# A depthwise convolution on VectorE: its two running sums get a PSUM bank each, and small operands move from SBUF to PSUM

## The chip, the cores and the metric

The kernel runs on one core of a Trainium2 chip. Its time is the device time of one execution in microseconds. TensorE, VectorE, ScalarE, GpSimd and SyncE each run their own instruction stream in order and meet through semaphores.

## What is computed

One inference step of a four-layer trunk, for a prompt of 512 tokens and for 8 samples of 4 tokens with shared weights, all in float32, D = 1024. Each layer is a mixer (pooling; Conformer convolution; chunked gating; short convolution) and a SwiGLU FFN of width 2816. The change is mostly in the second layer's mixer:

```python
def _rmsnorm(x, g):
    xf = x.astype(jnp.float32)
    y = xf * lax.rsqrt(jnp.mean(xf * xf, axis=-1, keepdims=True) + EPS)
    return (y * g.astype(jnp.float32)).astype(x.dtype)

def _conformer_conv(h, buf, w_in, b_in, dw, dw_b, ln_g, ln_b, w_out):
    z = jnp.einsum('bld,de->ble', h, w_in) + b_in
    a, gate = jnp.split(z, 2, axis=-1)
    g = a * jax.nn.sigmoid(gate)
    ext = jnp.concatenate([buf, g], axis=1)          # 30 earlier positions in front
    c = _depthwise_causal(ext, dw) + dw_b            # 31 taps per channel
    c = jax.nn.silu(_layernorm(c, ln_g, ln_b))
    return jnp.einsum('blc,cd->bld', c, w_out), ext[:, L:]

for i in range(DEPTH):
    h = _rmsnorm(x, norm_mix[i])
    x = x + mixer_i(h)
    x = x + _swiglu(_rmsnorm(x, norm_ffn[i]), ffn_w_in[i], ffn_w_out[i])
```

## The kernel before

Activations lie with channels on the 128 partitions and tokens along the free dimension: 8 chunks of 128 channels (`NC`), each with 544 token columns. The tokens are cut into half A (256 prompt tokens) and half B (256 prompt tokens and the 32 of the samples, 288 columns). Every float32 product is made of three matmuls from split operands: a rounded high part and the rest, `hi` and `lo`. Weights stream in through SyncE's queue (`raw`), ScalarE rounds them (`hi`, line 159), and VectorE or GpSimd subtracts (`lo`). Activations are split in the same way (`split`, `split_lo`: tiles `H_...`, `L_...`).

The order of each engine's instructions is that of the program text, which a planner writes: `Stream.run` walks over steps (a group of matmuls and its evacuation) and keeps a modelled clock per engine (`dve.t`, `pool.t`, `pe.t`; a VectorE instruction is taken to cost 0.07 us and 0.00104 us per element, `scalar_tensor_tensor` 0.065 more). Background jobs, the convolution's taps and norms among them, are generators that `background` advances after each step until `dve.t` reaches `pe.t` less a margin; a `yield None` waits for the next step. `settle` and `reached` hold a job back until the modelled clocks have passed. A step may also advance a job in its middle. `S.drain` issues what is left of the jobs.

The convolution of half A runs under the first layer's FFN of half B, and the convolution of half B under the second layer's FFN of half A. For each half:

- `conv_in` makes the gated inputs `ce` (tile `ext`) per chunk, 30 earlier columns in front; GpSimd clears or copies those columns. For half B `cs` holds the samples with their state.
- `conv_taps` adds 31 taps for the 256 prompt columns, in two running sums (even and odd taps) that lie in the two halves of one PSUM bank, `ct`. ScalarE writes the first tap of each; VectorE adds the other 29 with `scalar_tensor_tensor`, the last of the even ones into the SBUF tile `cc`, and then adds the odd sum to it. For the samples (half B), products with all 31 taps go into a bank `cw` and a `tensor_reduce` sums them; GpSimd adds the bias.
- GpSimd adds the finished `cc` of each chunk into `cm` (`accm`), for the mean over channels; the first chunk is copied there by ScalarE.
- `conv_norm` sums `cm` over partitions with a matmul (`cmean`), VectorE copies the mean to SBUF (`cmu`), subtracts it from each `cc`, ScalarE squares, GpSimd adds the squares (`cva`), and `token_rsqrt` makes the reciprocal root.

`token_rsqrt` sums over partitions into a bank `st_...`, so that tokens lie on partitions and a half has only two or three columns; `rsqrt_` then computes the root with shifts and Newton-like steps on VectorE in tiny SBUF tiles (`ms`, `ri`, `rt`); a matmul with the identity spreads the result over all partitions, into a bank `rp_...`. `scaled` has ScalarE copy that bank to SBUF (`r_...`, `cr`) with the constant factor `RSQ`. `Norm.prepare` then multiplies the eight chunks of x with the gain and `r` (`hn_...`), for the norms whose half is normalised before the matmuls (`pre`). The norms that take both halves at once use the same functions.

All PSUM tiles come from one pool of eight banks (`PS`, tag `ps`). A matmul group holds a bank from its first matmul to its evacuation.

In the profile, VectorE's and GpSimd's instructions carry line 102, that of the `Timed` helper, so they are told apart by tile.

Of the kernel before, what the change touches and what calls it, by code (L numbers as in the profile page):

```python
# [10 lines left out]
I32 = mybir.dt.int32  # L11
# [53 lines left out]
def trunk_kernel(  # L65
# [70 lines left out]
    def col(i):  # L136
        return colsT[:, i : i + 1]
# [200 lines left out]
            if gens:  # L338
                yield

    def rsqrt_(ms, shape_of, mk):

        wi, t = mk("ri"), mk("rt")
        wv, tv = shape_of(wi), shape_of(t)
        dve.tensor_scalar(wv.bitcast(I32), ms.bitcast(I32), 1, None, op0=ALU.logical_shift_right)
        dve.tensor_scalar(wv.bitcast(I32), wv.bitcast(I32), -1, 0x5F3759DF, op0=ALU.mult, op1=ALU.add)
        dve.tensor_mul(tv, wv, wv)
        dve.tensor_mul(tv, tv, ms)
        dve.scalar_tensor_tensor(wv, tv, -3.0, wv, op0=ALU.add, op1=ALU.mult)
        dve.scalar_tensor_tensor(tv, wv, 0.25, wv, op0=ALU.mult, op1=ALU.mult)  # L350
        dve.tensor_mul(tv, tv, ms)
        dve.scalar_tensor_tensor(tv, tv, -10.0 / 3, tv, op0=ALU.add, op1=ALU.mult)
        dve.scalar_tensor_tensor(wv, tv, 5.0, wv, op0=ALU.add, op1=ALU.mult)
        return wi

    def scaled(out, r):
        act.activation(out, r, AF.Copy, scale=RSQ)
# [1 line left out]
    def token_rsqrt(acc, halves, name, lag, mid=(None,)):  # L359

        bl = [b for b in range(5) if blocks[b][0] in halves]
        b0, b1 = bl[0], bl[-1] + 1
        ps = PS(f"st_{name}")
        ms = sp.tile([P, 5], F32, tag="nms", name=f"ms_{name}", bufs=2)
# [15 lines left out]
        rs = rsqrt_(  # L383
            ms[:, b0:b1], lambda t: t[:, b0:b1],
            lambda n: sp.tile([P, 5], F32, tag=f"n{n}", name=f"{n}_{name}", bufs=2),
        )
# [12 lines left out]

    class Norm:  # L400
# [277 lines left out]
    def pool_half(h):  # L678
# [15 lines left out]
        rs = rsqrt_(ms, lambda t: t, lambda n: sp.tile([P, nb], F32, tag=f"p{n}{h}", name=f"p{n}{h}"))  # L694
        if h == B:
            dve.tensor_scalar(rs, rs, RSQ, None, op0=ALU.mult)
        yield 2.5
# [148 lines left out]
    def conv_in(h, fill):  # L846
# [65 lines left out]
        for c in range(NC):  # L912
            la, lg = cols_of(w_cin[c], f"ci{c}_{h}", True)
            if c == 0:
# [5 lines left out]
            S.add([la], lambda wt, c=c: a_mm(wt, c), lambda ps, c=c: a_evac(ps, c),  # L920
                  fill=fill)

    def conv_taps(h, c, e, ev):
        w = HW[h]
        cc = cv[h][c] = T(f"cc_{h}_{c}")

        acc = PS(f"ct_{h}_{c}")
        outs = (acc[:, :HP], acc[:, HP : 2 * HP])
        for k in range(2):
            act.activation(  # L930
                outs[k], e[:, k : k + HP], AF.Identity, scale=col(C_DW + k * NC + c),
                bias=0.0 if k else col(C_DWB + c),
            )
        yield 0.0
        for k in range(2, CW):
            o = outs[k % 2]
            dve.scalar_tensor_tensor(
                cc[:, :HP] if k == CW - 1 else o, e[:, k : k + HP], col(C_DW + k * NC + c), o,
                op0=ALU.mult, op1=ALU.add,
            )  # L940
# [18 lines left out]
        if c == 0:  # L959
            accm[h] = T(f"cm_{h}")  # L960
            act.copy(accm[h][:, :w], cc[:, :w])
        else:
            pool.tensor_add(accm[h][:, :w], accm[h][:, :w], cc[:, :w])
        yield 0.7

    def conv_norm(h):
        w = HW[h]
        yield from settle()
        pm_ = PS(f"cmean_{h}")
        pe.matmul(pm_[:, :w], ones, accm[h][:, :w], start=True, stop=True)  # L970
        yield from reached()
        mu = T(f"cmu_{h}")
        dve.tensor_scalar(mu[:, :w], pm_[:, :w], 1.0 / D, None, op0=ALU.mult)
        av = T(f"cva_{h}")
# [12 lines left out]
        scaled(rs[:, :w], out[h][:, :w])
# [100 lines left out]
    def gm_norm():  # L1088
# [339 lines left out]
```

## Time and profile before

| | before |
|---|---|
| device time, median of 3 (lowest to highest) | 2260.37 us (2260.27 to 2268.2) |
| the profiled execution | 2267.77 us |
| its span, first to last instruction | 2266.1 us |
| mean granted TensorE clock in it | 0.982 |
| TensorE busy | 2185.4 us, 96% of the span |
| VectorE busy | 1361.7 us, 60% |
| ScalarE busy | 867.7 us, 38% |
| GpSimd busy | 541.0 us, 24% |

The profiled execution is one of the slower of those seen, 7.4 us over the median of the runs. The page gives shares and 40 slices of equal length; what follows also uses the busy time by stretch, the waits (who stood idle, until which instruction of which engine ended), the groups of like instructions and the timeline. An instruction's time in these views runs from its start to its end, and two on one engine can overlap a little.

### The profile page before, as it was taken

How to read it: one execution, taken by the hardware profiler on the slowest of the kernel's cores; microseconds unless marked ns; L12 is line 12 of the kernel's file. 1: busy time of each engine (PE TensorE's matmuls, PEld its weight loads, DVE VectorE, ACT ScalarE, POOL GpSimd, SP SyncE). 2: the span in 40 equal slices, each digit the busy share in tenths (PEclk: the TensorE clock that was granted, in tenths of full speed). 3: DMA queues.
4: the chain of work that ended last, by engine and by line, in shares of the span. 5: the costliest groups of instructions: out<-in, count | busy, mean ns of one | idle time of the engine just before them, and what ended most of it. 6: DMA issues, size and time to landing. Idle time of an engine off the chain costs nothing.

```text
span 2266.1 us, 41810 instructions
## 1 busy us (share of the span) xinstructions
PE 2185.4 (96%) x17110; PEld 2172.3 (96%) x17110; DVE 1361.7 (60%) x2569; ACT 867.7 (38%) x1407; POOL 541.0 (24%) x378
## 2 busy tenths in 40 slices
PE   9999988999788999999999999999999999999998
PEld 9999988999788899999999999999999999999998
DVE  6857789725999957566478543344465654433434
ACT  4445443454333465444434332232322233222322
POOL 3011666878667880000033000000000000000001
PEclk8999999999999999999999999999999999999999
DMA  6645543545654455555423322322344522232221
GB/s 228 219 146 165 170 140 113 176 151 170 144 151 140 167 168 171 152 190 149 141 79 126 106 83 70 110 92 68 93 89 95 94 84 94 67 97 98 88 71 60
DMA packets 112039, 284.07 MB, mean 125 GB/s; under 512 B 30540, under 2 KB 37800, under 8 KB 111584
## 3 DMA queue, kind: packets, MB, share of 16 engines
q1 hardware_dynamic: 110376, 279.47, 41.3%
q8 instruction: 134, 2.20, 0.4%
q10 hardware_dynamic: 1152, 1.32, 0.2%
q0 software_dynamic: 320, 0.62, 0.1%
q14 instruction: 57, 0.47, 0.1%
HBM read 277.11 MB, written 4.62 MB: 124 GB/s over the span
## 4 chain that ended last, share of the span: by engine, by line
PE 68%; DVE 10%; ACT 1%; issue 1%; DMA 1%; POOL 0%; DVEq 0%; POOLq 0%; ACTq 0%
PE ps_o L102 18%; PE ps_u L102 17%; PE ps_g L102 16%; DVE ct L102 3%; PE ps_gv L102 3%; PE ps_go L102 2%; PE ps_sc L102 2%; PE ps_sx L102 2%; PE ps_sbg L102 2%; PE ps_so L102 2%; PE ps_co L102 1%; DVE cw L102 1%; DVE cc L102 1%; DVE vT L102 1%; DMA raw_fi<-in_w_fin 0%
## 5 line engine op out<-in xcount | busy, mean ns | idle before, releaser
L102 DVE TENSOR_TENSOR lo_fi<-raw_fi,hi_fi 128x1024 fp32r<-128x1024 f32 (+1 forms) x180 | 222.1, 1236 | 333.2 <-issue 262.3
L159 ACT CAST hi_fi<-raw_fi 128x1024 fp32r<-128x1024 f32 x264 | 276.2, 1049 | 327.7 <-PE ps_g L102 108.3
L102 PE MATMUL ps_o<-H_p,lo_fo 128*128 128x288 f32 (+1 forms) x1408 | 354.8, 290 | 7.6 <-POOL lo_fo L102 7.6
L102 PE MATMUL ps_o<-H_p,hi_fo 128*128 128x288 f32 (+1 forms) x1408 | 355.7, 291 | 5.0 <-ACT H_p L507 5.0
L102 PE MATMUL ps_o<-L_p,hi_fo 128*128 128x288 f32 (+1 forms) x1408 | 355.5, 291 | 1.1 <-DVE L_p L102 1.0
L159 ACT CAST hi_fo<-raw_fo 128x768 fp32r<-128x768 f32 x192 | 150.0, 782 | 284.4 <-PE ps_o L102 150.1
L102 PEld LDWEIGHTS ps_o<-H_p,lo_fo 128*128 128x128 f32 x1408 | 249.7, 190 | 8.2 <-POOL lo_fo L102 8.2
L102 PEld LDWEIGHTS ps_o<-H_p,hi_fo 128*128 128x128 f32 x1408 | 250.0, 191 | 5.7 <-ACT H_p L507 5.7
L102 PEld LDWEIGHTS ps_o<-L_p,hi_fo 128*128 128x128 f32 x1408 | 250.0, 190 | 2.0 <-DVE L_p L102 2.0
L102 DVE TENSOR_TENSOR lo_fo<-raw_fo,hi_fo 128x768 fp32r<-128x768 f32 (+1 forms) x128 | 113.6, 890 | 226.3 <-issue 104.9
L102 PE MATMUL ps_u<-hH_f,hi_fi 128*128 128x256 f32 (+1 forms) x1040 | 242.4, 288 | 0.0
L102 PE MATMUL ps_g<-hH_f,hi_fi 128*128 128x256 f32 (+1 forms) x1040 | 242.4, 288 | 0.0
L102 PE MATMUL ps_g<-hL_f,hi_fi 128*128 128x256 f32 (+1 forms) x1040 | 242.4, 288 | 0.0
L102 PE MATMUL ps_u<-hL_f,hi_fi 128*128 128x256 f32 (+1 forms) x1040 | 242.3, 288 | 0.0
L102 PE MATMUL ps_g<-hH_f,lo_fi 128*128 128x256 f32 (+1 forms) x1040 | 241.7, 287 | 0.6 <-DVE lo_fi L102 0.6
L102 PE MATMUL ps_u<-hH_f,lo_fi 128*128 128x256 f32 (+1 forms) x1040 | 241.6, 287 | 0.0
L102 DVE SCALAR_TENSOR_TENSOR ct<-ce,colsT,ct 128x256 f32<-128x256 f32 x448 | 218.8, 488 | 24.3 <-ACT ct L930 11.2
L102 POOL TENSOR_TENSOR lo_fi<-raw_fi,hi_fi 128x1024 fp32r<-128x1024 f32 (+1 forms) x86 | 204.3, 2403 | 25.1 <-ACT hi_fi L159 21.5
L102 PEld LDWEIGHTS ps_g<-hH_f,lo_fi 128*128 128x128 f32 x1040 | 176.2, 188 | 0.8 <-DVE lo_fi L102 0.8
L102 PEld LDWEIGHTS ps_g<-hH_f,hi_fi 128*128 128x128 f32 x1040 | 176.2, 188 | 0.1
L102 PEld LDWEIGHTS ps_u<-hH_f,hi_fi 128*128 128x128 f32 x1040 | 176.2, 188 | 0.1
L102 PEld LDWEIGHTS ps_u<-hH_f,lo_fi 128*128 128x128 f32 x1040 | 176.2, 188 | 0.0
(346 smaller groups left out, 4922.6 us busy)
## 6 DMA issues: line engine op xcount, KB each, us to landing
raw_fi<-in_w_fin SPq DMA_DIRECT2D x264, 512.0 KB, 4.0
raw_fo<-in_w_fout SPq DMA_DIRECT2D x96, 384.0 KB, 3.2
raw_fo<-in_w_fout SPq DMA_DIRECT2D x96, 320.0 KB, 2.9
raw_ci<-in_w_cin SPq DMA_DIRECT2D x32, 512.0 KB, 4.0
raw_co<-in_w_cout SPq DMA_DIRECT2D x16, 512.0 KB, 4.8
raw_gi<-in_w_gin SPq DMA_DIRECT2D x16, 512.0 KB, 3.9
raw_go<-in_w_gout SPq DMA_DIRECT2D x16, 512.0 KB, 3.8
raw_si<-in_w_sin SPq DMA_DIRECT2D x16, 512.0 KB, 3.8
```

The costliest lines, as they stand in the source:

```text
L102: return fn(*a, **k)
L159: act.copy(self.hi, self.raw)
```

## The change

The convolution's two sums get a bank each, `ct0` and `ct1`. VectorE writes the first tap of each with `tensor_scalar`, with the bias in the first; ScalarE has no part in it any more. The two products for a pair of sample positions become one instruction of 2 × 8 × 31 elements, over a view with overlapping windows (`windows`). Adding a chunk to `cm` is put off (`late`) until the next chunk's twelfth tap has been issued; the last one is added at the start of `conv_norm`.

In `conv_norm` the mean is no longer copied: VectorE reads it from the bank `cmean` and scales and subtracts in one instruction. Each square is added one chunk later than before. In `conv_norm` and `Norm.prepare` the reciprocal root is read from its bank `rp_...` instead of an SBUF copy. The factor `RSQ` moves into that instruction or into a table of gains, which ScalarE scales once at the start (`gains`, 72 columns).

`rsqrt_` takes, for the norms of one half, two more column ranges in the bank `st_...` (`twin`). The two integer shifts stay in SBUF; of each later instruction at most one tensor operand is in SBUF, and three small copies keep both places filled. The norms of both halves and those of the first and third layers' mixers compute as before, except that the first shift writes the other of the two tiles.

```diff
-    def rsqrt_(ms, shape_of, mk):
-        wi, t = mk("ri"), mk("rt")
-        wv, tv = shape_of(wi), shape_of(t)
-        dve.tensor_scalar(wv.bitcast(I32), ms.bitcast(I32), 1, None, op0=ALU.logical_shift_right)
-        dve.tensor_scalar(wv.bitcast(I32), wv.bitcast(I32), -1, 0x5F3759DF, op0=ALU.mult, op1=ALU.add)
-        dve.tensor_mul(tv, wv, wv)
-        dve.tensor_mul(tv, tv, ms)
...
+    def rsqrt_(ms, wv, tv, twin=None):
+        wp, tp = twin or (wv, tv)
+        def copied(dst, src):
+            if twin:
+                dve.tensor_copy(dst, src)
+        dve.tensor_scalar(tv.bitcast(I32), ms.bitcast(I32), 1, None, op0=ALU.logical_shift_right)
+        dve.tensor_scalar(wv.bitcast(I32), tv.bitcast(I32), -1, 0x5F3759DF, op0=ALU.mult, op1=ALU.add)
+        copied(wp, wv)
+        dve.tensor_mul(tp, wv, wp)
+        dve.tensor_mul(tp, tp, ms)
+        dve.scalar_tensor_tensor(wp, tp, -3.0, wv, op0=ALU.add, op1=ALU.mult)
+        copied(wv, wp)
+        dve.scalar_tensor_tensor(tp, wp, 0.25, wv, op0=ALU.mult, op1=ALU.mult)
+        dve.tensor_mul(tp, tp, ms)
+        copied(tv, tp)
+        dve.scalar_tensor_tensor(tp, tp, -10.0 / 3, tv, op0=ALU.add, op1=ALU.mult)
+        dve.scalar_tensor_tensor(wv, tp, 5.0, wv, op0=ALU.add, op1=ALU.mult)
...
+        twin = (ps[:, 8 + b0 : 8 + b1], ps[:, 16 + b0 : 16 + b1]) if len(halves) == 1 else None
...
-            r = T(f"r_{nm}")
-            scaled(r[:, :w], out[h][:, :w])
+            r = out[h]
...
-                        v, x[h][:, i, :], col(self.g + i), r[:, :w], op0=ALU.mult, op1=ALU.mult
+                        v, x[h][:, i, :], gains[:, self.g + i : self.g + i + 1], r[:, :w],
+                        op0=ALU.mult, op1=ALU.mult,
...
+    act.activation(gains, colsT[:, :C_FIN], AF.Copy, scale=RSQ)
...
     def conv_taps(h, c, e, ev):
-        acc = PS(f"ct_{h}_{c}")
-        outs = (acc[:, :HP], acc[:, HP : 2 * HP])
-        for k in range(2):
-            act.activation(outs[k], e[:, k : k + HP], AF.Identity, scale=col(C_DW + k * NC + c), bias=...)
-        yield 0.0
-        for k in range(2, CW):
-            o = outs[k % 2]
-            dve.scalar_tensor_tensor(cc[:, :HP] if k == CW - 1 else o, e[:, k : k + HP], col(...), o, ...)
+        outs = [PS(f"ct{i}_{h}_{c}")[:, :HP] for i in range(2)]
+        for k in range(CW):
+            o = outs[k % 2]
+            wk = col(C_DW + k * NC + c)
+            src = e[:, k : k + HP]
+            if k == 0:
+                dve.tensor_scalar(o, src, wk, col(C_DWB + c), op0=ALU.mult, op1=ALU.add)
+            elif k == 1:
+                dve.tensor_scalar(o, src, wk, None, op0=ALU.mult)
+            else:
+                dve.scalar_tensor_tensor(cc[:, :HP] if k == CW - 1 else o, src, wk, o, op0=ALU.mult, op1=ALU.add)
+            if k == 11 and late:
+                late.pop()()
             if k % 2:
                 yield 0.8
...
-                for i in range(2):
-                    pv = b3(pr[:, i * DB * CW : (i + 1) * DB * CW])
-                    dve.tensor_mul(pv, ev[:, :, t + i : t + i + CW], taps)
+                pv = pr[:, : 2 * DB * CW].rearrange("p (i b k) -> p i b k", i=2, b=DB)
+                dve.tensor_mul(pv, windows(ev, t), taps)
...
-            pool.tensor_add(accm[h][:, :w], accm[h][:, :w], cc[:, :w])
+        late.append(gather)                  # gather() holds the copy or add into accm
...
     def conv_norm(h):
+        late.pop()()
...
-            dve.tensor_sub(cc, cc, mu[:, :w])
+            dve.scalar_tensor_tensor(cc, pm_[:, :w], -1.0 / D, cc, op0=ALU.mult, op1=ALU.add)
...
-            dve.tensor_mul(cc, cc, rs[:, :w])
+            dve.scalar_tensor_tensor(cc, cc, RSQ, out[h][:, :w], op0=ALU.mult, op1=ALU.mult)
```

More of the change, by code (lines that the diff above doesn't have):

```diff
@@ L366, in token_rsqrt @@
         ps = PS(f"st_{name}")
-        ms = sp.tile([P, 5], F32, tag="nms", name=f"ms_{name}", bufs=2)
+        ms, rs, tv = (sp.tile([P, 5], F32, tag=f"n{n}", name=f"{n}_{name}", bufs=2) for n in ("ms", "ri", "rt"))
+        twin = (ps[:, 8 + b0 : 8 + b1], ps[:, 16 + b0 : 16 + b1]) if len(halves) == 1 else None
         if B in halves:
@@ L382, in token_rsqrt @@
                 )
[L383 to L386, printed above, removed]
+        rsqrt_(*(t[:, b0:b1] for t in (ms, rs, tv)), twin)
         yield from lag
@@ L664, in trunk_kernel @@
     act.dma_start(colsT, par)
+    gains = cp.tile([P, C_FIN], F32, tag="gains", name="gains")
     wpool = [Load(w_pool[:, i], 1024, f"pool{i}") for i in range(2)]
@@ L693, in pool_half @@
         dve.scalar_tensor_tensor(ms, ms, EPS, mv[:, :, 1], op0=ALU.add, op1=ALU.add)
-        rs = rsqrt_(ms, lambda t: t, lambda n: sp.tile([P, nb], F32, tag=f"p{n}{h}", name=f"p{n}{h}"))
+        wv, tv = (sp.tile([P, nb], F32, tag=f"p{n}{h}", name=f"p{n}{h}") for n in ("ri", "rt"))
+        rs = wv
+        rsqrt_(ms, wv, tv)
         if h == B:
@@ L921, in conv_in, with windows @@
                   fill=fill)
+    late = []
+    def windows(ev, t):
+        v = ev[:, :, t : t + CW]
+        p, b, k = v.ap
+        return bass.AP(tensor=v.tensor, offset=v.offset, ap=[p, [1, 2], b, k])
     def conv_taps(h, c, e, ev):
@@ L925, in conv_taps @@
         cc = cv[h][c] = T(f"cc_{h}_{c}")
-        acc = PS(f"ct_{h}_{c}")
-        outs = (acc[:, :HP], acc[:, HP : 2 * HP])
-        for k in range(2):
[L930 to L933, printed above, removed]
-        yield 0.0
-        for k in range(2, CW):
-            o = outs[k % 2]
[L937 to L940, printed above, removed]
+        outs = [PS(f"ct{i}_{h}_{c}")[:, :HP] for i in range(2)]
+        for k in range(CW):
+            o = outs[k % 2]
+            wk = col(C_DW + k * NC + c)
[5 more added lines that the diff above has]
+            else:
+                dve.scalar_tensor_tensor(
+                    cc[:, :HP] if k == CW - 1 else o, src, wk, o, op0=ALU.mult, op1=ALU.add
+                )
+            if k == 11 and late:
+                late.pop()()
             if k % 2:
@@ L943, in conv_taps @@
         if ev is not None:
-            taps = colsT[:, C_DW + c : C_DW + CW * NC : NC].unsqueeze(1).to_broadcast([P, DB, CW])
+            taps = colsT[:, C_DW + c : C_DW + CW * NC : NC].unsqueeze(1).unsqueeze(1).to_broadcast([P, 2, DB, CW])
             for t in range(0, DS, 2):
                 pr = PS(f"cw_{c}_{t}")
-                for i in range(2):
-                    pv = b3(pr[:, i * DB * CW : (i + 1) * DB * CW])
-                    dve.tensor_mul(pv, ev[:, :, t + i : t + i + CW], taps)
+                pv = pr[:, : 2 * DB * CW].rearrange("p (i b k) -> p i b k", i=2, b=DB)
+                dve.tensor_mul(pv, windows(ev, t), taps)
                 dve.tensor_reduce(
                     b3(cc[:, HP:w]).rearrange("p b t -> p t b")[:, t : t + 2, :],
-                    pr[:, : 2 * DB * CW].rearrange("p (i b k) -> p i b k", i=2, b=DB),
+                    pv,
                     axis=mybir.AxisListType.X, op=ALU.add,
@@ L958, in conv_taps, with gather @@
         dve.tensor_add(cc[:, :HP], cc[:, :HP], outs[1])
[L959 to L962, printed above, removed]
-            pool.tensor_add(accm[h][:, :w], accm[h][:, :w], cc[:, :w])
+        def gather():
+            if c == 0:
+                accm[h] = T(f"cm_{h}")
+                act.copy(accm[h][:, :w], cc[:, :w])
+            else:
+                pool.tensor_add(accm[h][:, :w], accm[h][:, :w], cc[:, :w])
+        late.append(gather)
         yield 0.7
@@ L971, in conv_norm @@
         yield from reached()
-        mu = T(f"cmu_{h}")
-        dve.tensor_scalar(mu[:, :w], pm_[:, :w], 1.0 / D, None, op0=ALU.mult)
         av = T(f"cva_{h}")
-        sq = []
+        last = None
         for c in range(NC):
             cc = cv[h][c][:, :w]
-            dve.tensor_sub(cc, cc, mu[:, :w])
+            dve.scalar_tensor_tensor(cc, pm_[:, :w], -1.0 / D, cc, op0=ALU.mult, op1=ALU.add)
             s = av if c == 0 else T(f"csq_{h}_{c}")
             act.activation(s[:, :w], cc, AF.Square)
-            if c:
-                pool.tensor_add(av[:, :w], av[:, :w], s[:, :w])
+            if last is not None:
+                pool.tensor_add(av[:, :w], av[:, :w], last[:, :w])
+            last = s if c else None
             yield 0.4
+        pool.tensor_add(av[:, :w], av[:, :w], last[:, :w])
         yield from settle()
         out = yield from token_rsqrt({h: av}, (h,), f"cln_{h}", settle(), reached())
-        rs = T(f"cr_{h}")
-        scaled(rs[:, :w], out[h][:, :w])
         yield from reached()
@@ L1094, in gm_norm @@
         dve.tensor_scalar(ms, mv[:, :, 1], EPS, None, op0=ALU.add)
-        rs = rsqrt_(ms, lambda t: t, lambda n: sp.tile([P, 5], F32, tag=f"g{n}", name=f"g{n}"))
+        wv, tv = (sp.tile([P, 5], F32, tag=f"g{n}", name=f"g{n}") for n in ("ri", "rt"))
+        rs = wv
+        rsqrt_(ms, wv, tv)
         dve.tensor_scalar(rs, rs, RSQ, None, op0=ALU.mult)
```

6 lines of the change are left out of this document (removed).

## The prediction

> **What bounds the kernel now.** I read the page's shares and its 40 slices first.
>
> ```profile
> PE 2185.4 (96%) x17110; PEld 2172.3 (96%) x17110; DVE 1361.7 (60%) x2569; ACT 867.7 (38%) x1407; POOL 541.0 (24%) x378
> PE   9999988999788999999999999999999999999998
> DVE  6857789725999957566478543344465654433434
> POOL 3011666878667880000033000000000000000001
> PEclk8999999999999999999999999999999999999999
> ```
>
> TensorE is the bound over the whole, and no part of the change takes a convolution matmul away. What can be won are the slices where PE falls to 7 or 8. Most lie at slices 4 to 14, where VectorE shows 9 and GpSimd 6 to 8: the two convolutions under the FFN halves. Next, the busy time by stretch; each pair is busy us (instructions), then the granted clock:
>
> ```profile
> core 0: us, PE busy (x) PEld busy (x) DVE busy (x) ACT busy (x) POOL busy (x), PEclk, DMA share, GB/s
> 265.00:400.00 135.00, 119.39 (x866) 117.05 (x865) 121.67 (x267) 54.01 (x84) 89.97 (x57) 0.95 0.41 131
> 400.00:480.00 80.00, 76.76 (x567) 76.24 (x566) 51.17 (x74) 41.70 (x69) 63.57 (x33) 0.98 0.52 171
> 480.00:520.00 40.00, 40.00 (x304) 40.00 (x303) 5.51 (x12) 16.54 (x27) 31.08 (x20) 1.00 0.52 152
> 560.00:765.00 205.00, 172.86 (x1315) 170.43 (x1313) 190.31 (x365) 81.73 (x124) 139.31 (x87) 0.93 0.56 150
> 765.00:840.00 75.00, 71.29 (x566) 70.38 (x567) 51.16 (x66) 44.09 (x81) 64.86 (x37) 0.95 0.50 152
> 840.00:1160.00 320.00, 320.00 (x2467) 319.52 (x2466) 189.16 (x331) 145.64 (x227) 11.49 (x15) 1.00 0.50 156
> ```
>
> Where no convolution runs (840 to 1160) PE is full at clock 1.00. In W1, the taps of half A (265 to 400), it idles 135 − 119.4 = 15.6 us and loses 5% of 119.4 = 6.0 to the lower clock; it needs 113.4. In W2, the taps of half B (560 to 765), it idles 32.1 and loses 7% of 172.9 = 12.1; it needs 160.8. Together 65.8 us are lost, and VectorE is busy 90 and 93% there. The tails (400 to 480, 765 to 840) lose 3.2 + 1.5 and 3.7 + 3.6. That total, 78 us, is the ceiling.
>
> Then what PE waited for in W2 and, last three rows, around W1 (265 to 420): total, times, longest.
>
> ```profile
> PE ps_u L102 <- DVE cc L102: 9.1, 3, 4.5
> PE ps_gu L102 <- DVE ce L102: 8.3, 1, 8.3
> PE ps_o L102 <- POOL lo_fo L102: 4.3, 1, 4.3
> PE rp_f L102 <- DVE ri_f L102: 4.0, 1, 4.0
> ...
> PE ps_u L102 <- POOL lo_fi L102: 2.8, 1, 2.8
> PE ps_gu L102 <- POOL ce L102: 2.5, 1, 2.5
> PE ps_ca L102 <- POOL lo_ci L102: 1.1, 1, 1.1
> ```
>
> Half of W2 is VectorE late; in W1 it is GpSimd. But GpSimd is itself held, in order, by the channel sum `cm`, and each channel's taps begin with a wait for ScalarE (around W1, then in W2):
>
> ```profile
> POOL cm L102 <- DVE cc L102: 27.6, 6, 6.9
> POOL cm L102 <- PE ps_g L102: 6.4, 1, 6.4
> DVE ct L102 <- ACT ct L930: 7.2, 4, 2.5
> DVE ct L102 <- ACT ct L930: 4.0, 3, 1.6
> ```
>
> **The taps, each sum in its own bank.** VectorE's timeline and the groups by shape (busy us, mean ns, idle before):
>
> ```profile
> 339.66 4.17 DVE L102 SCALAR_TENSOR_TENSOR ct<-ce,colsT,ct 128x256 f32<-128x256 f32 x8 [1.52 <-ACT ct L930]
> 343.73 0.45 DVE L102 TENSOR_TENSOR L_p<-ps_u,H_p 128x288 fp32r<-128x288 f32 x1
> 344.10 3.10 DVE L102 SCALAR_TENSOR_TENSOR ct<-ce,colsT,ct 128x256 f32<-128x256 f32 x6
> ...
> L102 DVE SCALAR_TENSOR_TENSOR ct<-ce,colsT,ct 128x256 f32<-128x256 f32 x448 | 218.8, 488 | 24.3 <-ACT ct L930 11.2
> L102 DVE TENSOR_SCALAR sy<-se,colsT 128x256 f32<-128x256 f32 x16 | 5.6, 347 | 0.0
> ```
>
> Eight taps of 490 ns end after 4.17 us, so they start 525 ns apart: each begins 35 ns after the one before has ended. The unrelated `L_p` starts 4.07 us after the first tap, 4.07 − 7 × 0.525 = 0.395 after the last one, which is still running. So VectorE starts an instruction that needs nothing from its predecessor 0.13 us earlier. The sums alternate: tap k needs the result of k−2, and the only thing it shares with k−1 is the bank. With two banks, k−2 is 0.79 us back and has ended. How many pairs? The idle of the `ct` row without ScalarE's part is 24.3 − 11.2 = 13.1 us; at 35 ns that is 374 gaps, 187 per half. Each gives 0.127 us: 23.8 us per half.
>
> VectorE also takes on the first two taps, 16 × 2 instructions from SBUF into PSUM. No row has that form. The nearest, `sy`, is 0.35; with the overlap seen above it could be 0.26, and a full tap costs 0.40. I take 0.36: 5.8 us per half, bounds 4.2 and 6.4. By the Trainium skill, "VectorE: DVE Perf Modes", section "Why PSUM operands drop a tier", fp32 with PSUM runs one element per cycle; an estimate from its 0.96 GHz, 256 cycles, is 4.3 us per half before any fixed part. In return the waits for ScalarE go, 7.2 and 4.0. Late next is then whatever ScalarE waited for: the rows `ce` (VectorE's own, in order) and GpSimd's copy of the carried columns, priced below.
>
> **Sample products, norms, means.** These have in common that operands leave SBUF.
>
> ```profile
> L102 DVE TENSOR_TENSOR cw<-cs,colsT 128x248 f32<-128x248 f32 x32 | 28.9, 903 | 0.5
> L102 DVE TENSOR_TENSOR cw<-cs,colsT x32: 608/648/2658, 594.6 to 761.9; 128x248 f32<-128x248 f32 x32
> L102 DVE TENSOR_TENSOR cc<-cc,cmu 128x288 f32<-128x288 f32 x8 | 11.1, 1449 | 0.0
> L102 DVE TENSOR_TENSOR cc<-cc,cr 128x288 f32<-128x288 f32 x8 | 9.6, 1204 | 0.8 <-ACT cr L357 0.8
> L102 DVE SCALAR_TENSOR_TENSOR y<-xg,rp_nl 128x288 f32<-128x288 f32 x8 | 3.0, 446 | 1.9 <-PE rp_nl L102 1.9
> L102 DVE SCALAR_TENSOR_TENSOR hn_f<-x,colsT,r_f 128x256 f32<-128x256 f32 x8 | 5.7, 748 | 0.0
> 572.48 2.30 DVE L102 TENSOR_SCALAR ri_f<-ri_f 128x2 int32<-128x2 int32 x1
> 574.82 0.16 DVE L102 TENSOR_TENSOR rt_f<-ri_f 128x2 f32<-128x2 f32 x1
> 575.80 2.24 DVE L102 SCALAR_TENSOR_TENSOR rt_f<-rt_f 128x2 f32<-128x2 f32 x1
> ```
>
> Two columns take 0.16 us or 2.3, and `cc` 1.2 to 1.4 us where the same 288 columns with one PSUM operand (`y`) take 0.45. The long ones lie where GpSimd is busy; I read them as instructions held while GpSimd works on SBUF.
> - `cw`: two products become one of 496 columns. The pair costs 2 × 0.903 = 1.81. The new one lies between 0.9 (the time per column of the plain rows, plus one hold of 0.26) and 1.6 (2 × 0.648 plus that hold); I take 1.37, since 608 ns as the shortest of 248 columns says that it is slow by itself. 16 × 0.44 = 7 us in W2, bounds 3 and 14.
> - `hn_f` from PSUM: 748 to the taps' 488, eight times: 2.1 us in W2.
> - The norm at 572: the two shifts stay in SBUF, so the 2.30 stays; the 2.24 falls to 0.16; three copies of 0.2 are added: 1.5 us. Other one-half norms gain a hold or two, or lose 0.6 where GpSimd is idle; at the very start and end that may show, so −1 for all.
> - The means: `mu`'s instruction goes, and the 16 `cc` of a half fall to 0.45: 8 × (1.00 + 0.76) = 14 us of VectorE in B's tail, and as much in A's. PE loses only 12 us in both tails, so most of this is worth nothing; with two norms of `n1` nearby I take 5 us.
> - ScalarE loses 32 taps and a scale per norm; at 38% busy that shows nowhere but in the waits already counted. `gains` runs in a ScalarE that is idle until the first split: nothing, unless the parameter load lands late (0.5 us).
> - The banks of the norm are held for its eight products instead of one copy, and a channel holds two of eight banks instead of one; TensorE groups queue for the rest. In the sum nothing; a rival below.
>
> **GpSimd's sums later.** `cm` is issued after tap 11 of the next channel, some 5 us after what it reads is done. So the 27.6 + 6.4 us in which GpSimd stood before its `lo` splits go, and with them W1's waits for `lo_fi` and `lo_fo`. B's `cc` bias still follows the sample reduction at once, so there the queue stays held whenever VectorE is late. GpSimd's lateness at W1's start (`ce` 2.5, `lo_ci` 1.1) has no such cause and stays: with its share of the clock loss (6.0 on 15.6) 5 us.
>
> **The sum.** W1: VectorE is freed of 23.8 + 7.2 − 5.8 = 25.2 us and needs 110 where PE needs 113.4. PE leads again: its 21.6 lost us come back but for the 5, that is 16 us. W2: 23.8 + 4.0 + 7.0 + 2.1 + 1.5 − 5.8 = 32.6, VectorE still needs 172 against PE's 160.8 and sets the pace: 33 us. Tails and norms 5, copies −1: 53 us in all. The profiled execution took 2267.8 (span 2266.1); less 53 that is 2215. The median of the runs, 2260.4, is 7.4 lower, so I say 2207. With the bounds (taps −1 to +3, `cw` −4 to +7, tails 0 to 10) this case runs from 2190 to 2225.
>
> **Rivals.**
> 1. The 525 ns do not come from the bank: they are what dependent-looking instructions cost. The Trainium skill ("VectorE: DVE Perf Modes", "The DRAIN you can't avoid") says the next operation "does not start until the 8-stage pipe empties", semaphore or not. By that rule the 47.6 us of both halves stay. The `L_p` row, 0.395 us behind a tap of 490, speaks against it. Then W1 gains 7.2 − 5.8 = 1 us, W2 9, GpSimd's freed queue some 5, tails 4: 19 us, 2241.
> 2. Banks: `ps_u <- DVE cc` (9.1 us in 3) looks like TensorE waiting for a bank that the sums held. With one bank fewer it meets this more often, though VectorE, now on time, releases sooner. Eight more such waits of 3 us with the clock loss give back 30: 2237.
> 3. Slower: the same mechanism at every channel. A wait at 9.1 / 3 = 3.0 us plus 1.2 of lost clock, at both banks of 16 channels, is over 130 us; at one bank of each, 67: 2260 − 53 + 67 = 2274. It decides from 3.3 us per channel (53 / 16) on. Against it: before, PE shows three such waits in W2 and none around W1.
> 4. Better: VectorE's relief in W2 passes on whole and the clock stays up; nearly the ceiling of 78: 2182.
>
> **Chances.** Forecast 0.58; rival 1, 0.1; rival 2, 0.13; rival 3, 0.05; rival 4, 0.14. The range takes rivals 2 and 4 in: 2180 to 2240. 0.5%, or 11 us, is about what can be told from no change here; faster has rivals 1, 2, 4 and the forecast but for a rest near zero: 0.9, same 0.05, slower 0.05.
>
> **What would show it.** Taps start about 0.40 us apart and none waits for ScalarE; the two starting taps are near 0.36. In W1 and W2 PE at 95% or more and clock near 1.00, VectorE at 80 to 95%. No `cm` wait on VectorE; the `cc` bias wait remains, shorter. `cc` near 0.45, the norm's ten middle steps all at 0.16 with two shifts still long. Wrong if taps stay at 525 ns, if PE waits for `cc` grow, or if GpSimd's `lo` become what PE waits for in W2.

## The result and the profile after

| | before | after |
|---|---|---|
| median (lowest to highest) | 2262.51 us (2260.27 to 2268.2), 4 runs | 2192.11 us (2191.2 to 2195.81), 4 runs |
| ratio, 95% interval | | 0.9688 [0.9665, 0.9711] |
| profiled execution, its span | 2267.77, 2266.1 us | 2191.2, 2189.3 us |

The change takes 70 us off. The profile's page after the change, in the rows that the prediction showed of before:

```profile
PE 2156.0 (98%) x17110; PEld 2147.0 (98%) x17110; DVE 1298.7 (59%) x2613; ACT 851.4 (39%) x1372; POOL 542.7 (25%) x378
PE   9999999999999999999989999999999999999997
DVE  7867798517999566565587443344555554434444
POOL 3011787888788910000050000000000000000001
PEclk9999999999999999999999999999999999999998
```

TensorE's holes in slices 4 to 14 (the first slice is 0) are gone. The 9s of VectorE in slices 10 to 12 are the convolution of half B, where it is still the slower engine.

**By stretch.** The convolution is best cut at TensorE's own marks, since the stretches of fixed length shift. A runs from the first `ps_cga` matmul of half A to its first `ps_co` matmul, B from there to the first `ps_co` matmul of half B. Busy time by stretch, before and then after; the columns are the prediction's, and the first row of each pair is A:

```profile
238.98:527.82 288.84, 267.93 (x1988) 264.47 (x1987) 195.83 (x376) 128.94 (x201) 210.88 (x126) 0.97 0.47 150
527.82:848.55 320.73, 283.45 (x2197) 278.93 (x2196) 273.19 (x470) 145.09 (x236) 238.37 (x144) 0.95 0.55 154
```

```profile
232.33:491.83 259.50, 257.48 (x1989) 257.03 (x1987) 169.66 (x397) 122.07 (x184) 211.77 (x126) 1.00 0.53 167
491.83:773.28 281.45, 270.91 (x2197) 267.61 (x2195) 233.11 (x477) 135.47 (x216) 239.66 (x144) 0.99 0.62 175
773.28:2189.30 1416.02, 1399.07 (x11044) 1395.34 (x11042) 721.10 (x1396) 475.38 (x778) 51.61 (x65) 0.99 0.35 103
```

A gives 29.3 us, B 39.3, and what follows B 1.5 (1417.55 before): together 70. The two profiles differ by 6.7 us more, because the first convolution matmul came at 238.98 us before and at 232.33 after. Over all profiles of this study, whose code ahead of that point is nearly the same, it came between 231.4 and 239.0, so this is not counted as the change's. The late start would also account for the profiled execution of before lying 5.3 us above its median; the other executions left no profile. The 1.5 us behind B are within what the profiles of the experiments differ by there (1415.8 to 1419.6 us), so they cannot be called the change's either.

**By the prediction's stretches**, at the places to which they have moved and a little wider in matmuls: W1, A's tail, W2, B's tail, with what TensorE waited for longest in W2:

```profile
258.00:375.00 117.00, 117.00 (x908) 117.00 (x907) 112.60 (x287) 50.11 (x71) 97.13 (x60) 1.00 0.53 165
375.00:470.00 95.00, 95.00 (x722) 94.94 (x721) 39.61 (x77) 48.21 (x81) 74.43 (x39) 1.00 0.53 165
518.00:700.00 182.00, 172.57 (x1384) 170.73 (x1383) 176.29 (x372) 76.19 (x110) 148.56 (x88) 0.99 0.65 175
700.00:780.00 80.00, 78.88 (x648) 77.63 (x648) 44.60 (x79) 50.28 (x90) 68.13 (x43) 1.00 0.59 181
```

```profile
PE ps_gu L102 <- DVE ce L102: 2.8, 1, 2.8
PE ps_ca L102 <- DVE cc L102: 1.6, 1, 1.6
PE ps_g L102 <- DVE cc L102: 1.5, 1, 1.5
PE ps_g L102 <- POOL lo_fi L102: 1.4, 1, 1.4
```

W1 and A's tail lose nothing any more: TensorE is busy for 117.00 of 117 and 95.00 of 95 us at clock 1.00. W2 still loses 9.4 us of idle time and 1% of 172.6 to the clock, 11 in all, against 44 before; there VectorE is busy for 176 of 182 us. B's tail loses 1. So of the 78 us that the prediction called the ceiling, 66 came back; the other 3 of A's and B's gain lie ahead of W1 and W2.

**On VectorE.** Its timeline in half B's taps, and its groups by shape:

```profile
561.44 0.93 DVE L102 TENSOR_SCALAR ct<-ce,colsT 128x256 f32<-128x256 f32 x2
562.29 4.00 DVE L102 SCALAR_TENSOR_TENSOR ct<-ce,colsT,ct 128x256 f32<-128x256 f32 x10
566.20 0.23 DVE L102 SCALAR_TENSOR_TENSOR cs<-ps_ca,colsT,ct 128x32 f32<-128x32 f32 x1
...
L102 DVE SCALAR_TENSOR_TENSOR ct<-ce,colsT,ct 128x256 f32<-128x256 f32 x448 | 182.1, 480 | 0.0
L102 DVE TENSOR_TENSOR cw<-cs,colsT 128x496 f32<-128x496 f32 x16 | 28.6, 1790 | 0.0
L102 DVE TENSOR_SCALAR ct<-ce,colsT 128x256 f32<-128x256 f32 x32 | 14.9, 510 | 0.1
L102 DVE TENSOR_TENSOR L_cn<-cc,H_cn 128x256 fp32r<-128x256 f32 x8 | 11.5, 1450 | 2.7 <-ACT H_cn L512 2.7
L102 DVE SCALAR_TENSOR_TENSOR cc<-cc,rp_cln 128x288 f32<-128x288 f32 x8 | 3.4, 441 | 0.0
```

Ten taps fill 566.20 − 562.29 = 3.91 us: one starts every 0.391 us where it was 0.525, though each still lasts 0.48. The two starting taps fill 0.85 us.

### The profile page after: what moved, and what is told of

Read it like the earlier page. It is cut to its first block, busy times and chain, and to the rows that moved or that the text cites. A ratio compares the mean times of both kernels' runs of the same rounds, so it can differ in the third digit from the quotient of the medians.

```text
span 2189.3 us, 41838 instructions
## 1 busy us (share of the span) xinstructions
PE 2156.0 (98%) x17110; PEld 2147.0 (98%) x17110; DVE 1298.7 (59%) x2613; ACT 851.4 (39%) x1372; POOL 542.7 (25%) x378
## 4 chain that ended last, share of the span: by engine, by line
PE 83%; DVE 12%; DMA 2%; ACT 1%; issue 1%; POOL 1%; SPq 0%; DVEq 0%; POOLq 0%; ACTq 0%
PE ps_o L102 22%; PE ps_g L102 20%; PE ps_u L102 20%; DVE ct L102 4%; PE ps_gv L102 3%; PE ps_co L102 2%; PE ps_sc L102 2%; PE ps_sx L102 2%; PE ps_sbg L102 2%; PE ps_so L102 2%; DVE cw L102 1%; DMA raw_fi<-in_w_fin 1%; PE ps_go L102 1%; PE ps_cg L102 1%; DVE vT L102 1%
## 5 line engine op out<-in xcount | busy, mean ns | idle before, releaser
L159 ACT CAST hi_fo<-raw_fo 128x768 fp32r<-128x768 f32 x192 | 149.9, 782 | 287.1 <-PE ps_o L102 154.2
L102 DVE SCALAR_TENSOR_TENSOR ct<-ce,colsT,ct 128x256 f32<-128x256 f32 x448 | 182.1, 480 | 0.0
L102 PEld LDWEIGHTS ps_g<-hL_f,hi_fi 128*128 128x128 f32 x1040 | 175.9, 188 | 0.0
```

Of the source, the lines that this page charges most:

```text
L102: return fn(*a, **k)
L159: act.copy(self.hi, self.raw)
```

## The experiments

Medians are of four runs each (`shifts_psum`: five), the ratio is to before on the same chip, A and B are the lengths of the two stretches in the profile. After has A 259.5 and B 281.5.

| kernel | what it is | median us | ratio [95%] | A | B |
|---|---|---|---|---|---|
| `one_bank` | after, both sums in one bank | 2235.62 | 0.9881 [0.9854, 0.9908] | 281.1 | 300.0 |
| `banks_only` | before, two banks | 2221.92 | 0.9816 [0.9798, 0.9835] | 263.5 | 307.8 |
| `norms_sbuf` | after, norms as before | 2213.95 | 0.9782 [0.976, 0.9804] | 260.5 | 299.9 |
| `root_sbuf` | after, only the roots as before | 2200.91 | 0.9723 [0.9704, 0.9741] | 260.4 | 287.9 |
| `products_sbuf` | after, only `prepare`'s products as before | 2196.46 | 0.9698 [0.9678, 0.9718] | 259.6 | 285.6 |
| `means_sbuf` | after, only `conv_norm`'s mean and products as before | 2199.4 | 0.9716 [0.9695, 0.9737] | 259.5 | 281.9 |
| `cm_at_once` | after, channel sums at once | 2196.71 | 0.971 [0.9687, 0.9732] | 259.8 | 285.5 |
| `cw_split` | after, two sample products | 2199.93 | 0.9716 [0.9699, 0.9734] | 259.5 | 287.1 |
| `act_begins` | after, ScalarE begins the sums | 2198.68 | 0.9708 [0.969, 0.9727] | 260.5 | 281.8 |
| `shifts_psum` | after, the root's shifts through PSUM too | 2190.65 | 0.9678 [0.9661, 0.9695] | 259.5 | 279.1 |
| `samples_psum` | that, and samples read from PSUM | 2189.76 | 0.9677 [0.9661, 0.9693] | 259.5 | 273.2 |
| `samples_act` | that, and ScalarE begins the sums | 2185.97 | 0.9657 [0.9643, 0.9671] | 260.5 | 274.5 |

The intervals of `root_sbuf`, `products_sbuf`, `means_sbuf`, `cm_at_once`, `cw_split` and `act_begins` overlap that of after (0.9665 to 0.9711), so a median alone does not tell what these pieces cost. It is read from A and B, each from one profile. That A lies between 259.5 and 260.5 us in after and in all ten of its variants with two banks, and B within 0.4 us of after's in two of them, suggests how well they repeat.

**1. The bank alone taken back: `one_bank`.**

```diff
-        outs = [PS(f"ct{i}_{h}_{c}")[:, :HP] for i in range(2)]
+        acc = PS(f"ct_{h}_{c}")
+        outs = (acc[:, :HP], acc[:, HP : 2 * HP])
```

> The changed kernel with both running sums in the two halves of one bank again; VectorE still begins them. Theory 1, the bank itself holds the taps: they start 0.52 us apart again instead of 0.39, VectorE needs 16 x 23 x 0.13 = 48 us more in the two convolutions and TensorE stands for most of it: about 2192 + 45 = 2237. Rival, what mattered is that operands left SBUF and ScalarE no longer begins the sums: the taps stay near 0.39 us or the difference is hidden, 2192 to 2200.

Its timeline on VectorE, the two starting taps of a channel and eight taps in W1, and its two stretches:

```profile
276.45 1.06 DVE L102 TENSOR_SCALAR ct<-ce,colsT 128x256 f32<-128x256 f32 x2
...
302.68 4.16 DVE L102 SCALAR_TENSOR_TENSOR ct<-ce,colsT,ct 128x256 f32<-128x256 f32 x8
306.74 0.46 DVE L102 TENSOR_TENSOR ps_u<-ps_u,t 128x288 f32<-128x288 f32 x1
...
233.06:514.14 281.08, 264.51 (x1988) 260.70 (x1987) 191.07 (x397) 120.48 (x184) 211.01 (x126) 0.98 0.49 154
514.14:814.14 300.00, 278.62 (x2197) 275.10 (x2195) 245.27 (x478) 135.81 (x217) 235.10 (x144) 0.97 0.58 165
```

With an instruction of 0.488 us as the last of eight, the starts lie (4.16 − 0.488) / 7 = 0.525 us apart: the old spacing, with everything else of the change in place. 43.5 us of the 70 go with it, 21.6 in A and 18.5 in B. That the shared bank spaced the taps, and that this was the largest part, is shown. The trace also lists the semaphores that an instruction waits for, and with them it tells where the wait sits. The second starting tap needs nothing from the first. In `one_bank` all 16 of them wait for VectorE's own semaphore, the one that the first tap raises, and start 0.035 us after the first has ended; in after none of the 16 waits for it, and they start 0.09 us before that end. So it is the program that waits when the two sums share a bank. Whether a shared bank would hold the taps without that wait, no run shows.

**2. The bank alone given: `banks_only`.** To before's code, with ScalarE still beginning both sums:

```diff
-        acc = PS(f"ct_{h}_{c}")
-        outs = (acc[:, :HP], acc[:, HP : 2 * HP])
+        outs = [PS(f"ct{i}_{h}_{c}")[:, :HP] for i in range(2)]
```

> The kernel before with one edit: each sum has its own bank, ScalarE still begins both. Theory 1: taps 0.39 us apart, 48 us of VectorE freed, of which some is eaten by the waits for ScalarE at each channel and by GpSimd's held queue: 2262 - 35 to - 45, about 2222. Rival: 2255 to 2262. If the second bank costs TensorE waits, PE's waits for the sums (cc) rise from 11 us in all.

```profile
231.38:494.89 263.51, 258.69 (x1989) 257.49 (x1987) 178.11 (x376) 129.65 (x201) 211.62 (x126) 1.00 0.52 165
494.89:802.69 307.80, 281.96 (x2197) 277.29 (x2195) 265.42 (x470) 145.22 (x236) 240.65 (x144) 0.96 0.57 161
```

A gains 25.3 of its 29.3 us from this alone, B only 12.9 of its 39.3: in B VectorE is still busy for 265 of 308 us, and its other work has to shrink too. GpSimd's `cm` is issued as early here as before, yet its waits for `cc` in A fall from 27.6 to 11.9 us, and what TensorE waits in A falls from 20.8 to 4.8 us, none of it for `ce` or `lo_ci`: these waits were VectorE's lateness passed on. The waits for `cc` do not grow in B with the second bank (8.9 us, 11.4 in W2 before).

**3. The norms back in SBUF: `norms_sbuf`, and its three pieces.**

```diff
-        twin = (ps[:, 8 + b0 : 8 + b1], ps[:, 16 + b0 : 16 + b1]) if len(halves) == 1 else None
+        twin = (ps[:, 8 + b0 : 8 + b1], ps[:, 16 + b0 : 16 + b1]) if False else None
...
-            r = out[h]
+            r = T(f"r_{nm}")
+            scaled(r[:, :w], out[h][:, :w])
...
+        mu = T(f"cmu_{h}")
+        dve.tensor_scalar(mu[:, :w], pm_[:, :w], 1.0 / D, None, op0=ALU.mult)
...
-            dve.scalar_tensor_tensor(cc, cc, RSQ, out[h][:, :w], op0=ALU.mult, op1=ALU.mult)
+            dve.tensor_mul(cc, cc, rs[:, :w])
```

> The changed kernel with the norms and means as before: one-half norms compute in SBUF, ScalarE copies the reciprocal root and VectorE the mean to SBUF. By the prediction's terms this piece was worth 2.1 + 1.5 + 5 - 1 = 8 us: 2200. Rival, that these holds in VectorE's queue delay whole stages (the start of half A's convolution, both tails): 15 to 25 us, 2207 to 2217, with the loss between the stages rather than in the taps.

It costs 21.8 us, nearly all in B. B's first part, up to the end of half B's `conv_in`, in this kernel and then after:

```profile
492.95:585.83 92.88, 82.00 (x598) 80.17 (x597) 83.82 (x141) 38.98 (x61) 68.48 (x47) 0.94 0.62 158
```

```profile
491.83:569.82 77.99, 76.44 (x598) 76.04 (x597) 64.60 (x133) 38.15 (x59) 66.86 (x46) 1.00 0.71 181
```

That is the rival of the expectation by its size, 15 to 25 us, not the 8 us of the prediction's terms. The same 598 matmuls take 14.9 us more: 9.3 of idle time (92.88 − 82.00 against 77.99 − 76.44) and 5.6 because they run longer at the lower clock. VectorE is busy for 19.2 us more. Two groups of norm products in that part, in this kernel and then after:

```profile
L102 DVE SCALAR_TENSOR_TENSOR hn_n<-x,colsT,r_n 128x288 f32<-128x288 f32 x8 | 8.5, 1098 | 1.4 <-ACT r_n L364 1.4
L102 DVE SCALAR_TENSOR_TENSOR hn_f<-x,colsT,r_f 128x256 f32<-128x256 f32 x8 | 7.4, 968 | 0.0
```

```profile
L102 DVE SCALAR_TENSOR_TENSOR hn_n<-x,gains,rp_n 128x288 f32<-128x288 f32 x8 | 3.7, 504 | 0.4 <-PE rp_n L102 0.4
L102 DVE SCALAR_TENSOR_TENSOR hn_f<-x,gains,rp_f 128x256 f32<-128x256 f32 x8 | 3.4, 468 | 0.0
```

They account for 8.8 us, the steps of the two roots there for about 8 more (six long ones, of which after keeps two). The three pieces were then undone one at a time: `root_sbuf` with the first hunk, `products_sbuf` with the second and the old `hn_` product, `means_sbuf` with the rest.

> The changed kernel with only the reciprocal root of the one-half norms back in SBUF (nine instructions, no copies); products and means still read PSUM. The three pieces that norms_sbuf took back together cost 22 us. Theory, the roots are what hurts, since TensorE waited 3.6 us for one of them at a granted clock that then falls: 10 to 15 us of the 22, half B's conv_in (53.6 us) back to 62 or more. Rival, the eight products (hn 0.47 us against 0.97 to 1.10) carry it: 3 to 5 us here, 2196.

> The changed kernel with only the norm's eight products per half back on an SBUF copy that ScalarE makes; roots and means stay in PSUM. Theory of the roots: 2 x 4 us of VectorE and a ScalarE copy, 3 to 6 us, 2197. Rival of the products: 10 us or more, 2203. If neither this nor root_sbuf is above 2197, the means in the tails carry it.

> The changed kernel with only the means and scalings of the convolution's norm back on SBUF copies. Roots (half B's part 6 us longer) and products (4 us) leave 8 of the 18 us that half B lost in norms_sbuf. Theory, the three pieces add up: 8 us here, all in half B's FFN, 2200. Rival, they overlap, since a late root or product only delays what the next one would have delayed: 0 to 3 us, 2194.

The root of half A's FFN norm on VectorE, in `root_sbuf`, with two of GpSimd's subtractions, and then in after (some of the steps):

```profile
532.27 2.03 DVE L102 TENSOR_SCALAR rt_f<-ms_f 128x2 int32<-128x2 int32 x1
...
534.93 2.37 DVE L102 SCALAR_TENSOR_TENSOR ri_f<-rt_f,ri_f 128x2 f32<-128x2 f32 x1
...
537.54 2.22 DVE L102 TENSOR_TENSOR rt_f<-rt_f,ms_f 128x2 f32<-128x2 f32 x1
...
534.90 2.40 POOL L102 TENSOR_TENSOR lo_ci<-raw_ci,hi_ci 128x1024 fp32r<-128x1024 f32 x1 [0.62 <-ACT hi_ci L159]
537.40 2.34 POOL L102 TENSOR_TENSOR lo_ci<-raw_ci,hi_ci 128x1024 fp32r<-128x1024 f32 x1
```

```profile
530.53 2.25 DVE L102 TENSOR_SCALAR rt_f<-ms_f 128x2 int32<-128x2 int32 x1
532.82 0.17 DVE L102 TENSOR_SCALAR ri_f<-rt_f 128x2 int32<-128x2 int32 x1
...
534.82 0.16 DVE L102 SCALAR_TENSOR_TENSOR ri_f<-st_f,ri_f 128x2 f32<-128x2 f32 x1
```

The long steps of 534.93 and 537.54 end 0.02 us after the subtractions of GpSimd beside them, at 537.30 and 539.76. The same holds for every long root step: the 15 over 1.5 us in `root_sbuf`, the 14 in before and the 5 in after each end 0.015 to 0.028 us after an instruction of GpSimd has ended. This bears out the prediction's reading that GpSimd holds them. Which step is held depends on when GpSimd's next subtraction starts.

In B, the roots are worth 6.4 us (TensorE waits 3.2 us for `rp_f` in `root_sbuf`; after has no such wait), between what theory and rival gave them, the products 4.1, the means 0.4. The median of `means_sbuf` is 7.3 us above after's, but its runs spread from 2193.35 to 2204.56, the profiled one is the fastest of them, and its profile shows no loss in A or B, so nothing can be said from it. The pieces in B add to 10.9 us and together cost 18.4: by these profiles they reinforce each other. That VectorE, late from one norm, meets the next one later would fit; no run shows it, and it stays open.

**4. GpSimd's sums at once: `cm_at_once`.**

```diff
-        late.append(gather)
+        gather()
         yield 0.7
...
-        late.pop()()
```

> The changed kernel, but GpSimd's channel sum is issued at once after the chunk's last addition, as before. Theory a: GpSimd's queue stands before it in half A as before the change (34 us in all before) and its lo splits come late: half A loses about 10 us, half B 2 to 3, 2204. Theory b: with VectorE on time the wait is short and the queue's slack covers it: within 3 us of 2192.

The median is 4.6 us above after's; A is 0.3 us longer and B 4.0. GpSimd's waits for `cc` before its sums over A and B, in before, in this kernel and in after:

```profile
POOL cm L102 <- DVE cc L102: 29.0, 10, 6.9
```

```profile
POOL cm L102 <- DVE cc L102: 12.3, 9, 3.6
```

```profile
POOL cm L102 <- DVE cc L102: 0.8, 2, 0.5
```

Theory a is refuted: with VectorE earlier, the waits fall from 29.0 to 12.3 us without the later issue, and those left, all but 1 us of them in A, cost A next to nothing. Theory b holds for A but not for B. There `cm` hardly waits, so its wait is not what costs 4.0 us; TensorE waits 4.8 us in B for GpSimd's `lo` tiles, 1.8 in after, and runs longer at a clock of 0.98 against 0.99. Why they are later there is not shown.

**5. Two sample products again: `cw_split`.**

```diff
-                dve.tensor_mul(pv, windows(ev, t), taps)
+                for i in range(2):
+                    dve.tensor_mul(pv[:, i], ev[:, :, t + i : t + i + CW], taps[:, i])
```

> The changed kernel with the two sample products of a pair as two instructions again. One of 496 columns takes 1.08 us at the least and 1.79 in the mean; two of 248 took 0.61 and 0.90. If only the mean counts, nothing: 2192. If each instruction can be held once by GpSimd and the pair costs its own wait, 3 to 5 us: 2196. The prediction had 7 us for it.

B grows by 5.6 us and the median by 7.8. The tile `cw` in this kernel and then after (busy us and mean ns; shortest, median and longest ns):

```profile
L102 DVE TENSOR_TENSOR cw<-cs,colsT 128x248 f32<-128x248 f32 x32 | 34.0, 1062 | 0.6
L102 DVE TENSOR_TENSOR cw<-cs,colsT x32: 612/658/2749, 554.1 to 706.3; 128x248 f32<-128x248 f32 x32
```

```profile
L102 DVE TENSOR_TENSOR cw<-cs,colsT x16: 1078/1833/2644, 551.5 to 696.3; 128x496 f32<-128x496 f32 x16
```

The one of 496 columns is held far more often (median 1.83 us against a shortest of 1.08), and with its mean of 1.79 it is hardly shorter than the two of before, 2 × 0.903. But in the changed kernel the two are slower as well, 2 × 1.062 = 2.12 us: more of them are held there, though their median is still 0.66. So the merge saves 34.0 − 28.6 = 5.4 us of VectorE, and B changes by 5.6. The expectation that only the mean counts, and that it is the same, compared with the products of before and missed this.

**6. Who begins the sums: `act_begins`.**

```diff
-            if k == 0:
-                dve.tensor_scalar(o, src, wk, col(C_DWB + c), op0=ALU.mult, op1=ALU.add)
-            elif k == 1:
-                dve.tensor_scalar(o, src, wk, None, op0=ALU.mult)
+            if k < 2:
+                act.activation(o, src, AF.Identity, scale=wk, bias=0.0 if k else col(C_DWB + c))
```

> The changed kernel, but ScalarE writes the first tap of each sum, as before; the two banks stay. VectorE is freed of 32 starting taps (0.45 and 0.39 us apart, 13 us in all) and waits for ScalarE at some channels instead (11 us before the change). Theory a, moving the start to VectorE was needed: 2197 to 2203. Theory b, it is even: 2188 to 2196.

B differs by 0.3 us, A by 1.0. VectorE waits 7.0 us for ScalarE and saves the 14.9 of the starting taps. Moving the start to VectorE brought at most a few microseconds.

**7. Further along the same way.** `shifts_psum` lets the first integer shift write the second twin bank and the next one read it; `samples_psum` also has ScalarE copy the samples of a chunk into a bank, from which the products read; `samples_act` adds the edit of `act_begins`.

```diff
-        dve.tensor_scalar(tv.bitcast(I32), ms.bitcast(I32), 1, None, op0=ALU.logical_shift_right)
-        dve.tensor_scalar(wv.bitcast(I32), tv.bitcast(I32), -1, 0x5F3759DF, op0=ALU.mult, op1=ALU.add)
+        dve.tensor_scalar(tp.bitcast(I32), ms.bitcast(I32), 1, None, op0=ALU.logical_shift_right)
+        dve.tensor_scalar(wv.bitcast(I32), tp.bitcast(I32), -1, 0x5F3759DF, op0=ALU.mult, op1=ALU.add)
...
+            pe_ = PS(f"ce_{c}")
+            act.copy(pe_[:, : DB * LS], ev.rearrange("p b l -> p (b l)"))
+            evp = b3(pe_[:, : DB * LS])
...
-                dve.tensor_mul(pv, windows(ev, t), taps)
+                dve.tensor_mul(pv, windows(evp, t), taps)
```

> The changed kernel, and the two integer shifts of a one-half norm also have one operand in PSUM: the first writes the bank, the second reads it. Theory of the holds: 0.9 to 2.4 us each fall to 0.17, so some 3 us per norm, of which half B's conv_in shows 2 to 4: 2189. Rival, the integer forms are held whatever their memory: 2192.

> As shifts_psum, and ScalarE copies each chunk's samples with their state into a bank, so that the sample products have one operand in PSUM. Theory of the holds: the mean of 1.79 us falls to the 1.08 that is the shortest now, or to 0.62 if the slow columns too came from SBUF; half B's taps, where VectorE is busy 98%, gain 8 to 12 us less what the third bank costs: 2180 to 2184. Rival, banks: with three of eight banks held TensorE waits for cc and ct again, 2192 or more.

> As samples_psum, and ScalarE begins the sums. In the changed kernel that was even for half B (281.5 against 281.8 us). If VectorE still sets half B's pace, the 6.7 us that it is freed of there show in part, 2177 to 2182; if TensorE does, the waits for ScalarE at the chunks' starts make it 1 to 3 us longer than samples_psum.

The root in `shifts_psum`, and the sample products and the FFN part of B in `samples_psum`:

```profile
244.56 0.16 DVE L102 TENSOR_SCALAR st_n<-ms_n 128x2 int32<-128x2 int32 x1
244.76 0.16 DVE L102 TENSOR_SCALAR ri_n<-st_n 128x2 int32<-128x2 int32 x1
```

```profile
L102 DVE TENSOR_TENSOR cw<-ce,colsT x16: 1080/1136/1168, 551.7 to 691.6; 128x496 f32<-128x496 f32 x16
...
573.42:768.54 195.12, 191.81 (x1598) 190.91 (x1599) 151.65 (x337) 101.84 (x167) 168.36 (x97) 0.99 0.61 181
```

The shifts fall from 2.3 to 0.16 us and B by 2.4. With one operand in PSUM no sample product is held any more (longest 1.17 us), and B falls by 8.3 us against after. The medians do not follow: `samples_psum` was expected at 2180 to 2184 us, and its 2189.76 cannot be told from `shifts_psum`. The median of `samples_act` fits neither expectation, 2177 to 2182 us or above `samples_psum`; by A and B the second came true, 2.3 us longer. `samples_act` has the lowest median, 6.1 us under after's, but its interval and after's overlap by a little, and by A and B together (535.0 us) it is behind `samples_psum` (532.7). In the profile of the latter the first convolution matmul came 2.9 us later, at 235.88 against 232.96 us, and the part behind B took 3.1 us longer; no run tells why. So a version faster than after is likely, by 2 and 6 us by these medians and 8 and 6 by A and B; which of the two is the better is not told apart.

## Why the prediction was right, and where it was off

The forecast was 2207 us, a gain of 53; the gain was 70, inside the range, nearer to rival 4 than to the forecast. The case's own bounds add up to 2192 to 2217 us, not to the 2190 to 2225 that it states, so the result lies at their very end. Term by term:

| term of the sum | forecast | measured |
|---|---|---|
| W1 | 16 | 21.6 |
| W2 | 33 | 33 (44 lost before, 11 after) |
| tails and norms, copies | 5 − 1 | 11 |
| ahead of W1 and W2 (`conv_in`), and after B | 0 | 3 + 1.5 |

That W2 comes out at 33 twice is partly luck. Over the whole of B, undoing the bank costs 18.5 us, where the forecast gave it 23.8, and undoing the norms costs 18.4, where it gave them 3.6 in W2.

- *The taps.* Right. The overlap was read from one unrelated instruction, `L_p`, 0.395 us behind a tap; the taps came to 0.391. `one_bank` shows the cause. Rival 1 fell with them, since the next tap starts 0.09 us before the last has ended. The Trainium skill ("VectorE: DVE Perf Modes", "The DRAIN you can't avoid") has the next operation wait for the pipeline to empty, but adds that one which is not held starts earlier; rival 1 left this addition out, and the 0.391 against 0.48 agrees with it. The section "Two Vector instructions with no wait between them" says when an instruction is held, and agrees with the second starting tap, which lost its wait with the shared bank and starts early.
- *The starting taps.* 0.36 was forecast, 0.85 / 2 = 0.42 measured, at 510 ns each; 2 us in both halves together. The waits for ScalarE that go, 11.2 us, weigh about as much: the forecast had this step at near nothing, and `act_begins` agrees.
- *GpSimd's lateness at W1's start.* This step failed. The prediction left 5 us there because `ce` and `lo_ci` had "no such cause". After, W1 has no wait at all, and `banks_only`, which leaves GpSimd's order alone, already has A at 263.5. The lateness was VectorE's, one step further back: GpSimd's copies `cpre`, in order before its next `lo_ci`, waited 15.8 us for VectorE's `ce` before, 10.1 in `banks_only` and 6.9 in after. The same error made GpSimd's queue the reason for W1's `lo` waits: `cm_at_once` changes A by 0.3 us.
- *Norms.* The mis-sized term: 2.1 + 1.5 + 5 − 1 = 7.6 us were forecast, 21.8 measured. Three steps failed. The products `hn_n` of half B, 1.1 us each with SBUF operands and 0.5 after (4.8 us), were not itemised but left to the 5 us "with two norms of `n1` nearby", although that norm stands in B's `conv_in`, ahead of W2, a stretch that the forecast put at nothing. Of the roots only the step of 2.24 us at 575.80 was counted. In the profile of before the root of half B's `n1`, also ahead of W2, had two held steps besides its shift:

```profile
537.47 2.29 DVE L102 TENSOR_TENSOR rt_n<-rt_n,ms_n 128x3 f32<-128x3 f32 x1
540.49 2.32 DVE L102 SCALAR_TENSOR_TENSOR rt_n<-ri_n 128x3 f32<-128x3 f32 x1
```

Nor is it fixed which steps are held: in `root_sbuf` two were held besides the shift in the norm for which the forecast counted one. And the terms were VectorE's time alone: behind 9.3 us of idle TensorE came 5.6 us of lower clock.
- *Sample products.* A product of 1.37 us was forecast, 1.79 measured, against a pair of 1.81 before. Undoing the merge still costs 5.6 us in B, near the forecast 7, because the pair would take 2.12 us in the changed kernel. The value was nearly right by luck, its working was not.
- *Signs.* Taps 0.40 apart, `cc` near 0.45 (0.447 and 0.441), ten steps of the root at 0.16: all came. Of the two shifts one is long in each norm of B's first part (2.33 and 2.25 us), the other takes 0.44 or 0.17. The wait of GpSimd's bias for `cc` in B remains, shorter: 18.1 us, 36.5 before. `cm` waits 0.8 us for VectorE in all, as good as none. VectorE is busy for 96 and 97% of W1 and W2, above the 80 to 95% forecast, as the stretches got shorter.
- *Rivals 2 and 3.* TensorE's waits for `cc` in W2 fell from 11.4 us, 9.1 of them for `ps_u`, to 3.3; they did not grow, although a channel holds one bank more.

## What to carry to other kernels

Give two accumulators that alternate on VectorE a PSUM bank each and measure it; here that was the largest part of the gain. Look for instructions that start only after the one before has ended though they need nothing from it, and compare with an unrelated neighbour in the timeline. Where GpSimd works, try to keep at most one input tensor of a VectorE instruction in SBUF, even in two-column ones; the integer shifts, with one input, were held as long as they read and wrote SBUF. Price a hold by what TensorE loses behind it (idle time and then clock), in the stretch where it waits, not by VectorE's time. Compare a piece with the changed kernel that lacks it, not with the kernel before: the two sample products were slower there. When several engines are late together, ask first whether they follow from one: here TensorE's waits for GpSimd in A fell from 14.0 to 1.9 us in `banks_only`, which leaves GpSimd's order as it was.

## What the runs showed of the hardware

- A hold that is taken from one instruction can appear at another. With the norms' operands out of SBUF, `L_cn` of half A, two operands in SBUF, rose from 0.78 to 1.45 us; with only the convolution's norm back on SBUF copies (`means_sbuf`) it took 0.87. A sample product of 248 columns, the same in all three, took 0.90 us on average in before, 1.22 in `banks_only` and 1.06 in `cw_split`. The Trainium skill ("SBUF — State Buffer", "Who interferes with whom") says that a VectorE instruction with two SBUF inputs contends with a GpSimd instruction that reads SBUF, and one with at most one, outside the two-port modes, does not. The long root steps with two inputs in SBUF end with GpSimd's subtractions and agree, and so do the sample products: 1.79 to 1.13 us on average when one operand moved to PSUM. The shifts, 2.3 to 0.16, have only one tensor input, so by this rule they would be held only if they ran in such a mode; no run shows in which they ran.
- Not held, the 496 columns with overlapping windows still take 1.08 us at the least, 2.2 ns per column, where the 288 of `cc` take 0.441, 1.5 ns per column. No run tells what makes the difference.
- A `tensor_scalar` from SBUF into PSUM takes 0.51 us for 256 columns, where the one from SBUF to SBUF took 0.347 and a tap with two tensor operands takes 0.48.
